# Half of the attention's gate as the first fill beside the last mixer's keys' chain, and the self-attention's rows in another tile

## The chip, the cores and the metric

One Trainium2 chip, one core. The metric is the time of one execution on the device in microseconds; each version is run several times and the median counts.

## The reference, cut to what matters

The whole model is one program: a first block of two layers (recurrent and attention mixers, cross-attention to a memory, MLPs), then a second block: a hybrid mixer and a mixture of 16 experts chosen by the experts. The change lies in the hybrid mixer. There are 256 positions of width 1024; the attention has 8 query and 2 key heads of 64, the delta rule 8 heads of 64 in both directions.

```python
proj = h @ w_in
aq, ak, av, dq, dk, dv, dz, b_raw, a_raw, g_raw = jnp.split(proj, ...)
# self-attention
q = axial_rope(rmsnorm_2(heads(aq, 8), q_norm_w), row, col)
k = axial_rope(rmsnorm_2(heads(ak, 2), k_norm_w), row, col)
attn = block_attention(q, k, heads(av, 2))
# delta rule, forward and backward, in chunks of 64
cq, ck, cv = jnp.split(silu(short_conv(concatenate([dq, dk, dv]), conv_w)), 3)
qd, kd = l2norm(heads(cq, 8)) * 64 ** -0.5, l2norm(heads(ck, 8))
o = rmsnorm_2(o_fwd + o_bwd, dn_norm_w) * silu(dz)
# two gates, then the output
gate_a, gate_d = jnp.split(sigmoid(g_raw), 2)
merged = gate_a * (attn @ w_attn_up) + gate_d * (dn @ w_dn_up)
x = x + gt1 * (merged @ w_o)
```

## The kernel before, in words

A dense product runs as three passes of split operands (L391, L392 and L393: high times high, low times high, high times low); a "dense row" below is one such matmul. Each weight tile of 1 MB comes through SP's queue into a ring of buffers named raw, and is split by ScalarE (L374, whi) and VectorE (L375, wlo). Features stand on the partitions (dense_fm_steps: 128 features by 256 positions) or positions do (dense_tm_steps).

mixer2 (L1184) does the hybrid mixer in four stretches, from about 830 to 1106 us.

- *The keys' chain.* The keys of the delta rule are convolved on TensorE (L1299), squared and summed per head (L1321), normed by Newton steps on VectorE (newton, L458 to L473), scaled (L1330) and transposed (L1335). Beside that decay() makes masks of decays (matmul L1352, multiplication L1357), and products() multiplies keys with keys (L1370) and with the masks (L1374).
- *The inverse*, for two pairs of chunks, pair_a and pair_b (inverse_steps). Each of four levels is a matmul (L1616, in each()), a multiplication on VectorE (L1642), a second L1616, and its result copied by ScalarE (L1646) and transposed by VectorE (L1647); the next level needs both. A last level is L1659 and L1667.
- *The recurrence* over the chunks (rec_steps: L1716 to L1754).
- *The end*: O is normed (L1779 to L1790), transposed (L1793), and goes through w_dn_up; then mixer2_out multiplies by w_o.

These are chains of small steps. All other work of the mixer is a chain of generators, `fill`, pulled at lower priority by counts between the steps of the chains (FILL_K, FILL_A, FILL_B, FILL_R), or up to a flag (until). In order, before: the projection of the delta rule's queries (project(0), with a convolution of sixteen multiply-adds L1181 on VectorE and L1302) and their norm (heads_normed(0): L1317, L1321, newton, L1330, L1335); the projection of self-attention's rows (its epilogue ez3 writes zq); the queries' masks and products; gains_loaded(), which loads the group p2 into finr and makes gt1; rotary() (L1405 to L1440), which reads zq and tab; the values (ev, with eight more L1181); the attention's gate (ega writes a tanh into m1), mixed with attend() (L1453 to L1479); the scaled queries; the attention's up-projection (ea); the two gates of the delta rule; and final_gain(), which multiplies X by finr (L1560). The framework's scheduler sets the final order on each engine from the order of issue and the priorities.

Behind the mixer the experts' weights follow, 192 loads of 1 MB named wx on the same SP queue, each into the next buffer that comes free.

finr and gt1 are two halves of the tile zT, whose earlier contents are used up by then. zq and tab are views of m1, the tile into which the gate is written later.

Of the kernel before, what the change touches and what calls it, by code (L numbers as in the profile page):

```python
# [47 lines left out]
MIX = 3  # L48
# [256 lines left out]
def _body(ctx, tc, I, lay, out, stop):  # L305
# [127 lines left out]
    def dense_tm_steps(W, c0, ncols, a, emit, kc=8, step=512, part=1024):  # L433
        ah, al = a
        for g0 in range(c0, c0 + ncols, step):
            wd = min(step, c0 + ncols - g0)
            kt = 2048 // step
            ws = [weights(W.load(k0 * P, kt, g0, wd), kt, wd, part=part) for k0 in range(0, kc, kt)]
            if step == 256:
                ps = bank_mm().rearrange("p (t n) -> p t n", t=2)  # L440
                ps = [ps[:, t, :] for t in range(2)]
            else:
                ps = [bank_mm() for _ in range(2)]
            for k in range(kc):
                wh, wl = ws[k // kt](k % kt, 0, wd)
                for t in range(2):
                    sl = slice(t * P, (t + 1) * P)
                    mm3(ps[t][:, :wd], ah[:, k, sl], al[:, k, sl], wh, wl, k == 0 and (t == 0 or step != 256),
                        k == kc - 1)
                if k < kc - 1:  # L450
                    yield
            for t in range(2):
                emit(t, g0 - c0, wd, ps[t][:, :wd])
            yield
# [546 lines left out]
    fill = Fill()  # L1001
# [182 lines left out]
    def mixer2(pool, norms):  # L1184
# [6 lines left out]
        W = weight("w_in_2")  # L1191
# [7 lines left out]
        def sc(nm, *shape):  # L1199
            return pool.tile([P] + list(shape or (2, 16)), F32, name=nm)  # L1200

        heads_up.pop()
        a = ah, al = features_tiles()

        rows = act.tile([P, 8, S + 2], F32, name="zT").rearrange("p c t -> p (c t)")
        finr, gt1 = rows[:, 0:D], rows[:, D:2 * D]

        shk = sc("shk", 4)
        for j in range(4):
            nc.scalar.copy(shk[:, j:j + 1], keys[j][:, S:S + 1])  # L1210
# [11 lines left out]
        m1 = pool.tile([P, 8, S], F32, name="m1")  # L1222
# [151 lines left out]
                nc.vector.tensor_tensor(m, hd(ps)[:, 4 * t:4 * t + 4, :], m, OP.mult)  # L1374


        flat = m1.rearrange("p c t -> p (c t)")
        zq = flat[:, 0:1280].rearrange("p (t n) -> p t n", t=2)
        tab = flat[:, 1280:1792].rearrange("p (k t d) -> p k t d", k=4, t=2)
        qT, kT, zv = (held[7][:, a:b].rearrange("p (c t) -> p c t", c=c)  # L1380
                      for a, b, c in ((0, 1024, 4), (1024, 1536, 2), (1536, 1792, 2)))
        sq8 = sc("sq8", 20)
# [142 lines left out]
        def ega(c, nb, ps):  # L1525
            nc.scalar.activation(m1[:, c:c + nb, :], ps, AF.Tanh, scale=0.5)
# [10 lines left out]
        def attention_inside():  # L1537
            for t in range(2):
                for d in range(2):
                    decay(d, t, 1)  # L1540
                    yield
            for hp in range(2):
                products(1, hp)
                yield

        def flag(name):
            done.add(name)
            return
            yield

        def gains_loaded():
            load_group(None, "p2", nc.sync, finr)

            gain_rows(2, 0.5, gt1)
            return
            yield
# [6 lines left out]
        def mix(p, q, n):  # L1563

            for _ in q:
                yield
                for _ in range(n):
                    if next(p, 0) is None:
                        yield
            yield from p  # L1570

        fill = chain(project(0), heads_normed(0),
                     dense_tm_steps(W, 0, 768, a, ez3, step=256), attention_inside(), flag("aT"), gains_loaded(),
                     rotary(), dense_fm_steps(W, 1792, 512, a, ev), flag("v"),
                     mix(dense_fm_steps(W, 2848, 1024, a, ega), attend(), MIX),
                     scaled_queries(), flag("qg"),
                     dense_fm_steps(weight("w_attn_up_2"), 0, D, (at[:, :4, :], at[:, 4:, :]), ea, kc=4),
                     dense_tm_steps(W, 2304, 512, a, ez, step=256), final_gain(),
# [605 lines left out]
```

## Time and profile before

| what | value |
|---|---|
| median of 3 runs | 1592.44 us (1588.39 to 1595.42) |
| profiled execution: its time / its span | 1594.02 / 1592.2 us |
| mean granted TensorE clock | 0.972 |
| TensorE busy | 1452.9 us (91% of the span) |
| VectorE busy | 853.0 us (54%) |
| ScalarE busy | 615.0 us (39%) |
| chain that ended last | TensorE 66%, DMA 25%, VectorE 5%, ScalarE 3% |

Shares are means over stages with different limits. The 25% of DMA in the chain are the experts' weights in the last 470 us; ahead of these the chain is TensorE's nearly throughout. What the change touches is some 280 us of the span, the mixer, so the stretch is read and not the mean.

### The profile page before, as it was taken

To read this page: it belongs to the slowest core of one execution; us is meant where nothing else is said; L and a number is where in the kernel's file an instruction comes from. 1 tells how busy PE (TensorE), PEld (TensorE's weight loads), DVE (VectorE), ACT (ScalarE), POOL (GpSimd) and SP (SyncE) were. 2 spreads that over 40 slices of the span, in tenths; PEclk is the share of its full clock that TensorE was granted. 3 is DMA by queue.
4 is the path that set the end of the run, shared out by engine and by line. 5 is a ranking of instruction groups with operands and counts; after the bars stand their busy time and mean duration, and the time that the engine had idled before them with its cause. 6 is when DMAs were issued, how large, how long until landed. Compare 5 with 4: busy or idle time off the path is not lost.

```text
span 1592.2 us, 25448 instructions
## 1 busy us (share of the span) xinstructions
PE 1452.9 (91%) x10592; PEld 1079.3 (68%) x10592; DVE 853.0 (54%) x1563; ACT 615.0 (39%) x1027; POOL 56.0 (4%) x69
## 2 busy tenths in 40 slices
PE   8999999999999999999999899999988786776776
PEld 8988898889887778898888788899834111111111
DVE  7785667877566766877566986556632001001001
ACT  6655545444445555644444456533311000000000
POOL 0000200000000020000002100010000000000000
PEclk9989999999999999999999999999998997998997
DMA  8535436876553334787544222436899999999998
GB/s 305 208 119 183 158 137 226 314 282 219 187 182 108 106 133 146 271 292 290 191 164 152 81 82 81 151 117 214 350 392 422 423 424 422 422 424 424 422 424 359
DMA packets 58772, 398.23 MB, mean 250 GB/s; under 512 B 6816, under 2 KB 7968, under 8 KB 12064
## 3 DMA queue, kind: packets, MB, share of 16 engines
q1 hardware_dynamic: 57168, 393.10, 64.2%
q10 hardware_dynamic: 1488, 3.49, 0.6%
q8 instruction: 83, 1.36, 0.3%
q14 instruction: 33, 0.27, 0.0%
HBM read 395.52 MB, written 1.05 MB: 249 GB/s over the span
## 4 chain that ended last, share of the span: by engine, by line
PE 66%; DMA 25%; DVE 5%; ACT 3%; issue 1%; SPq 0%; DVEq 0%; ACTq 0%
DMA raw<-in_wx_dram 24%; PE mm L391 14%; PE mm L393 14%; PE mm L392 14%; PE acc L392 3%; PE acc L393 3%; PE acc L391 3%; PE acc L1616 2%; DVE wlo L375 1%; PE mm L1983 1%; PE acc L1983 1%; DMA fraw<-in_w_ada_dram 1%; PE acc L549 1%; ACT whi L374 1%; PE mm L930 1%
## 5 line engine op out<-in xcount | busy, mean ns | idle before, releaser
L375 DVE TENSOR_TENSOR wlo<-raw,whi 128x1024 fp32r<-128x1024 f32 (+1 forms) x299 | 362.4, 1215 | 181.1 <-ACT whi L374 174.4
L374 ACT CAST whi<-raw 128x1024 fp32r<-128x1024 f32 (+1 forms) x299 | 309.6, 1040 | 345.9 <-PE mm L392 170.8
L391 PE MATMUL mm<-hTh,whi 128*128 128x256 f32 x1064 | 300.8, 286 | 6.6 <-ACT whi L374 6.2
L393 PE MATMUL mm<-hTh,wlo 128*128 128x256 f32 x1064 | 301.4, 286 | 4.9 <-DVE wlo L375 4.9
L392 PE MATMUL mm<-hTl,whi 128*128 128x256 f32 x1064 | 302.5, 287 | 0.0
L391 PEld LDWEIGHTS mm<-hTh,whi 128*128 128x128 f32 x1064 | 203.1, 192 | 11.3 <-ACT whi L374 6.2
L393 PEld LDWEIGHTS mm<-hTh,wlo 128*128 128x128 f32 x1064 | 203.6, 192 | 7.9 <-DVE wlo L375 6.8
L392 PEld LDWEIGHTS mm<-hTl,whi 128*128 128x128 f32 x1064 | 203.6, 192 | 1.9 <-issue 1.1
L1983 PE MATMUL mm<-raw,xe 128*32 128x512 f32 x504 | 109.3, 614 | 31.2 <-DMA raw<-in_wx_dram 31.2
L1983 PE MATMUL acc<-raw,xe 128*32 128x512 f32 x512 | 97.5, 608 | 19.1 <-DMA raw<-in_wx_dram 19.1
L1983 PEld LDWEIGHTS mm<-raw,xe 128*32 128x32 f32 x504 | 22.8, 111 | 113.6 <-DMA raw<-in_wx_dram 72.8
L2119 ACT ACTIVATE sgl<-acc 128x512 f32<-128x512 f32 x8 | 4.7, 597 | 215.1 <-PE acc L1983 215.1
L1983 PEld LDWEIGHTS acc<-raw,xe 128*32 128x32 f32 x512 | 21.4, 110 | 89.4 <-DMA raw<-in_wx_dram 51.2
L391 PE MATMUL acc<-whi,hh 128*128 128x512 f32 x192 | 75.7, 394 | 0.0
L392 PE MATMUL acc<-wlo,hh 128*128 128x512 f32 x192 | 75.7, 395 | 0.0
L393 PE MATMUL acc<-whi,hl 128*128 128x512 f32 x192 | 75.0, 394 | 0.0
L2120 DVE SCALAR_TENSOR_TENSOR sgl<-sgl,acc 128x512 f32<-128x512 f32 x8 | 5.4, 686 | 110.2 <-ACT sgl L2119 110.2
L1049 DVE SCALAR_TENSOR_TENSOR macc<-fraw,cs,macc 128x1024 f32<-128x1024 f32 x40 | 51.3, 1282 | 21.5 <-DMA fraw<-in_w_ada_dram 21.2
L2003 DVE SCALAR_TENSOR_TENSOR sgl<-sgl,mm 128x512 f32<-128x512 f32 x8 | 5.5, 688 | 106.0 <-PE mm L1983 105.9
L2016 PE MATMUL acc<-raw,xe 128*32 128x512 f32 x256 | 40.4, 738 | 22.6 <-DMA raw<-in_wx_dram 22.5
L393 PE MATMUL mm<-whi,hTl 128*128 128x256 f32 (+2 forms) x192 | 58.8, 308 | 0.7 <-DVE hTl L554 0.7
L392 PE MATMUL mm<-wlo,hTh 128*128 128x256 f32 (+2 forms) x192 | 58.8, 308 | 0.4 <-DVE wlo L375 0.4
(563 smaller groups left out, 2601.9 us busy)
## 6 DMA issues: line engine op xcount, KB each, us to landing
raw<-in_wx_dram SPq DMA_DIRECT2D x191, 1024.0 KB, 19.8
raw<-in_mlp_w_up_dram SPq DMA_DIRECT2D x32, 1024.0 KB, 5.0
raw<-in_mlp_w_down_dram SPq DMA_DIRECT2D x32, 1024.0 KB, 5.1
fraw<-in_w_ada_dram SPq DMA_DIRECT2D x22, 1024.0 KB, 6.7
raw<-in_w_in_dram SPq DMA_DIRECT2D x19, 1024.0 KB, 4.9
raw<-in_xa_w_kv_dram SPq DMA_DIRECT2D x16, 1024.0 KB, 4.9
raw<-in_ab_w_in_dram SPq DMA_DIRECT2D x9, 1024.0 KB, 8.6
raw<-in_xa_w_q_dram SPq DMA_DIRECT2D x8, 1024.0 KB, 4.7
```

The costliest lines, as they stand in the source:

```text
L374: nc.scalar.copy(hi[:, a:b], raw[:, c0 + a:c0 + b])
L375: (nc.gpsimd if len(parts) in slow else nc.vector).tensor_sub(lo[:, a:b], raw[:, c0 + a:c0 + b], f(hi[:, a:b]))
L391: mm(o, lh, rh, start=start, stop=False, skip_group_check=True)
L392: mm(o, lh, rl, start=False, stop=False, skip_group_check=True)
L393: mm(o, ll, rh, start=False, stop=stop, skip_group_check=True)
L549: mm(o[j * 64:j * 64 + 64, q0:S], v[:, k, vcol:vcol + 64], pT[:, c0:c0 + S - q0], start=k == 0, stop=k == 1, skip_group_check=True)
L930: mm(pss[s][:, c0:c1], qk[rs, qc, q0:q0 + P], qk[rs, kcs[s], 0:kn], start=True, stop=True)
L1049: nc.vector.scalar_tensor_tensor(acc[:, sl], w, ck, acc[:, sl], OP.mult, OP.add)
L1616: mm(o[J, c], lh[J, c], rh[J, c], start=True, stop=True)
L1983: mm(banks[n][j * 32:(j + 1) * 32, :], xe[:, c, g0 + j * 32:g0 + (j + 1) * 32], raw[:, e * D + n * 512:e * D + (n + 1) * 512], start=c == ...
L2003: nc.vector.scalar_tensor_tensor(sg[:, sl], sg[:, sl], 0.5, bu[n], OP.mult, OP.mult)
L2016: mm(by[j * 32:(j + 1) * 32, :], hT[:, c + k, j * 32:(j + 1) * 32], raw[:, k, j, :], start=c + k == 0, stop=c + k == 7, tile_position=(0, ...
```

## The change: what it does

The attention's gate has 1024 features. Its first half (w_in's columns 2848 to 3359) moves from beside attend() to the very front of the fill, ahead of the queries' projection. The second half stays beside attend(). The first half writes m1's first four chunks, which zq and tab occupy at that time before; so these two move to the first 1792 columns of `rows`, the tile zT. There finr and gt1 stand later, so gains_loaded(), which fills these, moves behind rotary(), the last reader of zq. No operation is added or left out.

```diff
         finr, gt1 = rows[:, 0:D], rows[:, D:2 * D]
+        zqt = rows[:, 0:1792]
...
-        flat = m1.rearrange("p c t -> p (c t)")
-        zq = flat[:, 0:1280].rearrange("p (t n) -> p t n", t=2)
-        tab = flat[:, 1280:1792].rearrange("p (k t d) -> p k t d", k=4, t=2)
+        zq = zqt[:, 0:1280].rearrange("p (t n) -> p t n", t=2)
+        tab = zqt[:, 1280:1792].rearrange("p (k t d) -> p k t d", k=4, t=2)
...
-        fill = chain(project(0), heads_normed(0),
-                     dense_tm_steps(W, 0, 768, a, ez3, step=256), attention_inside(), flag("aT"), gains_loaded(),
-                     rotary(), dense_fm_steps(W, 1792, 512, a, ev), flag("v"),
-                     mix(dense_fm_steps(W, 2848, 1024, a, ega), attend(), MIX),
+        fill = chain(dense_fm_steps(W, 2848, 512, a, ega), project(0), heads_normed(0),
+                     dense_tm_steps(W, 0, 768, a, ez3, step=256), attention_inside(), flag("aT"),
+                     rotary(), gains_loaded(), dense_fm_steps(W, 1792, 512, a, ev), flag("v"),
+                     mix(dense_fm_steps(W, 3360, 512, a, lambda c, nb, ps: ega(4 + c, nb, ps)), attend(), MIX),
```

Lines of the changed kernel are two higher than before from L1208 to L1377, and one higher behind that. The counts of pulls are unchanged.

On TensorE, at the end of the keys' chain, this is the order before (L1352 decays, L1335 the keys' transposes, L1370 keys' products, L1317 the queries' transposes; the dense rows behind are self-attention's):

```order
L1352 MATMUL acc<-w_8670,raw_8439 128x512
L1352 MATMUL acc<-w_8678,raw_8439 128x512
L1335 MATMUL tp<-ident,raw_8441 128x128 x4
L1352 MATMUL acc<-w_8857,raw_8439 128x512
L1335 MATMUL tp<-ident,raw_8441 128x128 x4
L1370 MATMUL acc<-raw 64x64 x16
L1317 MATMUL tp<-ident,raw_8435 128x128 x2
L1370 MATMUL acc<-raw 64x64 x16
L1317 MATMUL tp<-ident,raw_8435 128x128 x2
L391 MATMUL mm<-whi,hTh 128x256
L1317 MATMUL tp<-ident,raw_8435 128x128 x4
L391 MATMUL mm<-whi,hTh 128x256
```

and this of the changed kernel, from the same L1352 on (L1354, L1337, L1372; the dense rows are the queries'):

```order
L1354 MATMUL acc<-w_8670,raw_8439 128x512
L1337 MATMUL tp<-ident,raw_8441 128x128 x8
L1354 MATMUL acc<-w_8678,raw_8439 128x512
L1354 MATMUL acc<-w_8827,raw_8439 128x512
L1372 MATMUL acc<-raw 64x64 x32
L391 MATMUL mm<-hTh,whi 128x256
L392 MATMUL mm<-hTl,whi 128x256
```

The queries' L1317 have left this place. The dense rows ahead of it are 96 in both: the queries' before, the gate's first half now.

At the end of pair_a's inverse on TensorE, before (L1616 two levels, with 34 dense rows between them, of which two are shown, then L1659 the last level):

```order
L1616 MATMUL acc<-w_9820,w_9625 64x64 x16
L1616 MATMUL acc<-w_9749,raw_8431 64x64 x16
L1440 MATMUL tp<-ident,raw_8437 128x128
L1440 MATMUL tp<-ident,raw_8435 128x128 x2
...
L391 MATMUL mm<-hTh,whi 128x256
L392 MATMUL mm<-hTl,whi 128x256
L1616 MATMUL acc<-w_9914,w_9750 64x64 x16
L1659 MATMUL acc<-w_9839,raw_8431 32x32 x16
L1496 MATMUL tp<-ident,wf 128x128 x4
```

and in the changed kernel (L1617 for L1616, L1337 and L1372 the queries' transposes and products, L1437 self-attention's transposes, L1660 and L1668 the last level):

```order
L1617 MATMUL acc<-w_9793,w_9557 64x64 x16
L1617 MATMUL acc<-w_9695,raw_8431 64x64 x16
L1337 MATMUL tp<-ident,wf 128x128 x8
L1372 MATMUL mm<-raw 64x64 x16
L1437 MATMUL tp<-ident,raw_8437 128x128
L1617 MATMUL acc<-w_9899,w_9696 64x64 x16
L1660 MATMUL acc<-w_9812,raw_8431 32x32 x16
L1372 MATMUL mm<-raw 64x64 x15
L1668 MATMUL acc<-w_9961,w_9813 32x32 x16
L1660 MATMUL acc<-w_9918,raw_8431 32x32 x16
```

The dense rows between the last levels have gone, and the queries' small matmuls stand there.

On VectorE, between the last two transposes of pair_a's inverse, before (L1647 the transposes, L1181 the values' convolution, L1642 the level's multiplication):

```order
L1647 STREAM_TRANSPOSE w_9840<-acc 128x512
L1181 SCALAR_TENSOR_TENSOR wf<-raw_8443,p_8452,wf 128x256 x2
L1642 TENSOR_TENSOR w_9914<-acc,raw_8439 128x512
L1181 SCALAR_TENSOR_TENSOR wf<-raw_8443,p_8452,wf 128x256 x2
L1175 MEMSET raw_8443 128x2x2
L375 TENSOR_TENSOR wlo<-raw,whi 128x1024
L1492 SCALAR_TENSOR_TENSOR wf<-wf 128x512
L1647 STREAM_TRANSPOSE w_9934<-acc 128x512
```

and in the changed kernel (L1648 and L1643 the same, L1561 final_gain()'s product, L1411 to L1433 rotary()):

```order
L1648 STREAM_TRANSPOSE w_9813<-acc 128x512
L1643 TENSOR_TENSOR w_9899<-acc,raw_8439 128x512
L470 TENSOR_TENSOR nw_a<-nw_y,ss_9562 128x20
L1561 TENSOR_TENSOR X<-X,zT 128x1024 x2
L471 SCALAR_TENSOR_TENSOR nw_b<-nw_a,nw_y 128x20
L473 SCALAR_TENSOR_TENSOR nw_y<-nw_b,nw_y 128x20
...
L473 SCALAR_TENSOR_TENSOR nw_y<-nw_b,nw_y 128x20
L1411 TENSOR_SCALAR sq_8565<-nw_y 128x20
...
L1433 COPY raw_8435<-raw_8435 128x64
L1648 STREAM_TRANSPOSE w_9919<-acc 128x512
```

The values' convolution has gone behind the last transpose, and final_gain()'s two products of 1024 columns and the end of rotary() stand ahead of it.

At the mixer's end the order holds 117 dense rows before between the last L1751 of the recurrence and the first L1793, and 64 in the changed kernel. On SP's queue the load of p2 stood ahead of nine loads of w_in before and stands behind them now, ahead of the four loads of w_attn_up.

## Rows read from the trace of the kernel before

**Rows 1.** TensorE's waits, 850 to 1130 us: who, for whom, total us, times, longest.

```profile
PE tp L1335 <- DVE raw L1330: 2.2, 1, 2.2
PE tp L1317 <- DVE raw L1302: 1.9, 1, 1.9
...
PE tp L1472 <- ACT raw L532: 1.2, 1, 1.2
```

**Rows 2.** Busy time by stretch: us, then PE, PEld, DVE, ACT, POOL, PEclk, DMA share, GB/s.

```profile
870.00:895.00 25.00, 20.06 (x165) 15.88 (x164) 22.03 (x54) 14.38 (x25) 3.00 (x2) 0.87 0.13 44
895.00:950.00 55.00, 54.74 (x864) 49.59 (x863) 48.56 (x107) 25.18 (x44) 4.90 (x4) 0.99 0.30 103
```

**Rows 3.** The same view behind the mixer, two stretches.

```profile
1110.00:1114.00 4.00, 4.00 (x36) 4.00 (x35) 3.27 (x5) 2.63 (x3) 0.00 (x0) 1.00 0.00 2
1200.00:1300.00 100.00, 81.82 (x430) 26.54 (x426) 13.23 (x34) 8.11 (x18) 0.00 (x0) 0.90 1.01 422
```

**Rows 4.** Timeline of TensorE, 874 to 904 us: start, us, line, tile.

```profile
874.16 1.02 PE L1352 MATMUL acc<-w,raw 128*128 128x512 f32 x2
...
882.65 1.91 PE L1352 MATMUL acc<-w,raw 128*128 128x512 f32 x2
...
901.24 1.15 PE L1616 MATMUL acc<-w,raw 64*64 64x64 f32 x32
```

**Rows 5.** Timeline of VectorE, 870 to 906 us.

```profile
872.57 0.53 DVE L1324 TENSOR_SCALAR ss<-ss 128x16 f32<-128x16 f32 x1
...
881.00 1.29 DVE L1330 TENSOR_TENSOR raw<-raw,ss 128x512 f32<-128x512 f32 x2
...
904.96 0.18 DVE L471 SCALAR_TENSOR_TENSOR nw_b<-nw_a,nw_y 128x16 f32<-128x16 f32 x1
905.17 0.18 DVE L473 SCALAR_TENSOR_TENSOR nw_y<-nw_b,nw_y 128x16 f32<-128x16 f32 x1
```

**Rows 6.** VectorE by line, 845 to 950 us: count, busy us, mean ns, idle before.

```profile
L375 DVE TENSOR_TENSOR wlo<-raw,whi 128x1024 fp32r<-128x1024 f32 x13 | 15.9, 1221 | 3.1 <-ACT whi L374 3.1
L1181 DVE SCALAR_TENSOR_TENSOR raw<-raw,p 128x256 f32<-128x256 f32 x16 | 7.1, 476 | 0.0
L1647 DVE STREAM_TRANSPOSE w<-acc 128x512 f32<-128x512 f32 x8 | 5.7, 712 | 3.7 <-ACT w L1646 3.7
...
L1181 DVE SCALAR_TENSOR_TENSOR wf<-raw,p,wf 128x256 f32<-128x256 f32 x8 | 3.4, 475 | 0.2 <-ACT wf L1179 0.2
...
L1374 DVE TENSOR_TENSOR raw<-mm,raw 128x256 f32<-128x256 f32 x8 | 2.9, 416 | 0.0
...
L1560 DVE TENSOR_TENSOR X<-X,zT 128x1024 f32<-128x1024 f32 x2 | 2.4, 1224 | 0.2 <-DMA zT<-in_p_dram 0.2
...
L1429 DVE TENSOR_TENSOR raw<-raw,nw_y 128x128 f32<-128x128 f32 x2 | 1.0, 482 | 0.0
...
L1431 DVE COPY raw<-raw 128x64 f32<-128x64 f32 x2 | 0.7, 342 | 0.0
```

**Rows 7.** VectorE from the keys' norms to the first pair's end, as in rows 2.

```profile
871.00:950.00 79.00, 73.80 (x1018) 64.47 (x1017) 70.15 (x159) 38.56 (x67) 7.91 (x6) 0.96 0.25 86
```

**Rows 8.** Timeline of TensorE at the mixer's end.

```profile
1087.70 1.14 PE L1751 MATMUL acc<-w,raw 64*64 64x64 f32 x16
...
1100.03 0.28 PE L391 MATMUL mm<-hTh,whi 128*128 128x256 f32 x1
1100.15 0.28 PE L392 MATMUL mm<-hTl,whi 128*128 128x256 f32 x1
...
1102.91 1.03 PE L1793 MATMUL tp<-ident,w 128*128 128x128 f32 x8
```

**Rows 9.** Timeline of VectorE at the mixer's end.

```profile
1095.48 1.23 DVE L375 TENSOR_TENSOR wlo<-raw,whi 128x1024 fp32r<-128x1024 f32 x1 [0.74 <-ACT whi L374]
...
1100.01 1.28 DVE L1790 TENSOR_TENSOR w<-w,wf 128x512 f32<-128x512 f32 x2
```

**Rows 10.** Transfers of 840 to 1000 us: count, KB, median us to landing.

```profile
zT<-in_p_dram SPq DMA_DIRECT2D x1, 512.0 KB, 3.5
```

## Prediction

> **What bounds the kernel now.** I read the windows first, stage by stage, to see where a microsecond is worth a microsecond. Behind the mixer the experts' weights bind: 423 GB/s and a DMA share of 1.01 while TensorE is four fifths busy, but at 1110 to 1114 us the same share is 0.00 [rows 3]. The stream cannot start before the mixer and the output product have given back their weight buffers. So a shift of the mixer's end passes on to the end one for one, as long as no load is brought forward.
>
> Inside the mixer TensorE binds: 54.7 of 55 us at 895 to 950. The exception is the keys' chain at 870 to 895, where TensorE is busy for 20.1 of 25 us and VectorE for 22.0, at a granted clock of 0.87 [rows 2]. The waits name the places: 2.2 us before L1335 (the keys' transposes, for VectorE's L1330) and 1.9 us before L1317 (the queries' transposes, for L1302) [rows 1]. In all TensorE idles 4.9 us in that window, 25 less 20.1. The timeline shows what the clock does behind an idle: a pair of L1352 takes 1.02 us at 874 and 1.91 us just behind the 2.2 us wait [rows 4]; that is the lower of the two levels, 1.2 GHz. A mean of 0.87 over 25 us means some 6.5 us at that level, and half of it is lost, 3.3 us. So the keys' chain loses **8.2 us** in all. That is all this change can win there.
>
> Why is L1330 late? VectorE's timeline: the Newton steps of the keys' norm begin behind L1324 at 872.57, and L1330 starts at 881.00, 8.4 us later. Undisturbed, Newton steps follow each other every 0.21 us [rows 5]. Between them stand the queries' sixteen convolution steps L1181, 7.1 us [rows 6].
>
> **The change part by part.** No operation is added or removed; the sum of matmul time between the mixer's ends is the same. Only places move.
>
> *Keys' chain.* The first gate half stands where the queries' projection stood: the same 96 dense rows, ahead of the same L1352. It has no VectorE epilogue (one tanh on ScalarE), so the sixteen L1181 and one L1302 leave the Newton steps. From 872.57: L1324 0.5, eleven steps of 0.21, one L1357 of 0.7, and hand-over: L1330 starts at about 876.5 to 877 instead of 881.0. Then the rest of the chain (L1352, the eight transposes, ScalarE's copies, L1370) still has no dense row among it. Going through it row by row leaves TensorE about 1.8 us idle, and the second wait, for L1302, is gone. **Gain 8.2 − 1.8 = 6.4 us**, bounded by 8.2 (no idle) and 4.
>
> *First inverse.* The queries' VectorE work is not gone. It stands in the first pair's inverse, in which every L1616 waits for VectorE's L1642 or L1647. That stretch was full already: 70.2 of 79.0 us from 871 to 950 [rows 7]. Counting by the order what stands ahead of the last L1647: eight L1181 of the values (3.4), eight L1374 (2.9), L1492 (0.65, as each L1330 [rows 5]) and two small copies (0.2 each) leave, 7.4 in all; two L1560 (2.4, which stood in an idle place before) and one L375 (1.2) come in [rows 6]. That leaves 66.4 us of work. With the old 8.8 us of gaps the last L1647 would end 3.8 us earlier than before: the **lower bound** of the sum for both parts, and a gain.
>
> The upper one comes from the last three steps. Before, 27 to 34 dense rows stood between two steps of the inverse on TensorE, and VectorE had 5 to 6 us of work per step; each covered the other. Now the last three steps hold 11 dense rows, then none. VectorE between the last two L1647 has L1560 2.4, L1429 1.0, the copies L1431 and L1432 some 1.3, ten small steps of 0.21, and L1642 with L1647 1.4 [rows 5, 6]: about 8 us. TensorE has beside it two L1616 of 1.1 [rows 4], the queries' transposes and products, and L1659: about 4.8. So it waits 3.2 us; the same sums for the two steps ahead (6.9 against 4.3, 8.9 against 6.7) give 2.6 and 2.2. **Cost 8.0 us**, at TensorE's most exposed. Both parts together: −6.4 + 8.0 = **+1.6**, between −3.8 and +2. I take the upper end, because the order gives TensorE nothing to do in these steps. The lower needs the gaps not to grow while the covers shrink.
>
> *Attention.* Half of the gate was the filler beside attend(); now 96 dense rows stand there, not 192, and they run out in the first of four rounds. The one wait of that kind was 1.2 us (L1472 for ScalarE's softmax) [rows 1]; I expect one more, of that size or a little less: **+0.8**, from 0 to 2.
>
> *Tail.* The last recurrence step (L1751) ends at 1088.84; the norm chain on ScalarE and VectorE lets L1793 begin once the first L1790 is done, at 1100.65 [rows 8, 9]. That is 11.8 us, under 117 dense rows of 0.12 us [rows 8], 13.9 us: no wait before. Now 64 rows are left, 7.6 us. The chain has the same three L375 in it; 0.7 us of it is a wait for ScalarE's cast that TensorE sets [rows 9], and may go. So TensorE waits 11.8 − 0.7 − 7.6 = **3.5 us** in front of L1793, bounded by 0 (if the recurrence itself runs ahead) and 4.2. Behind L1793 stand the delta rule's up-projection and then the output product, whose buffers the stream waits for.
>
> *The load of p2 (zT, 512 KB).* On SP's queue it moves behind nine weight loads and waits for the last reader of zq, and the four loads of the attention's up-projection stand behind it. It lands 3.5 us after its start [rows 10]. By the order VectorE has some 6 us of work between that reader and L1560. So it costs nothing; without that cover it would stall VectorE up to 3.5 us in the inverse. The rows' new place costs nothing: tile zT is free until then, and the writes and reads keep their sizes.
>
> *Clock behind the new idles.* Waits of 2.2 and 1.9 us cost 3.3 us by the lower level in the keys' chain. The new ones of 2.2 to 3.5 us may do the same, but behind them stand small matmuls: 0 to 3.4 us, taken as 0.5.
>
> The Trainium skill (Perfetto Trace Analysis, Matmul Optimizations) says that the matmul engine scales its power with its use, so that matmuls should run back to back. By that rule alone, closing the chain's two waits would be worth the whole 8.2 us, and 1592 would become 1584. The trace agrees with its mechanism (a pair of L1352 at 1.91 against 1.02 us), but the rule counts only the waits that close, and the order opens others; its result is the full gain among the rivals.
>
> **Sum.** +1.6 + 0.8 + 3.5 + 0.5 = +6.4 us on the profiled 1594.0, which stands 1.6 above the median 1592.4. On the median that is 1598.8. Three of four terms are at the exposed end, so I take a little off: **1598 us**.
>
> **The rivals.** A difference of 8 us (0.5%) is about what this kernel's measurement can tell from none.
> - *Covers hold (faster side).* The inverse's gaps stay at 8.8 us: −3.8, the recurrence runs ahead so that the tail does not wait, attention +0: 1588 to 1589. For it: VectorE really has less work there. Against: 64 rows for a chain of 11 us. To gain over 8 us it would need the whole 8.2 with nothing given back: 1584. Decides: the wait before the last L1659 is under 1 us.
> - *All waits exposed and the clock falls behind each (slower side).* +2.0, +2 in attention, +4.2, +3.4 of clock: +11.6, 1604. For it: the two waits of before both did it. Decides: granted clock under 0.9 behind the inverse and at L1793.
> - *The p2 load is late.* 3.5 us more on VectorE in the inverse: 1601 to 1602. Against: the cover of 6 us.
> - *Nothing arrives, since the stream binds.* If weight buffers, not the mixer, set its start, the time stays 1592. Against: the share of 0.00 at 1110.
>
> **Chances.** Forecast (+3 to +8) 0.45; covers hold in part or whole (−4 to +3) 0.25, a full gain over 8 us 0.05; all exposed 0.15; late load 0.05; nothing arrives 0.05. Of the forecast's 0.45 I put 0.1 over 8 us, since a median of three runs moves by 3 us. So slower by over 0.5%: 0.1 + 0.15 + 0.05 = 0.30; faster: 0.05; same: 0.65. The range is 1588 (covers hold) to 1604 (all exposed).
>
> **What would show it.** Right: L1330 at about 877 and no wait for L1302; waits of over 2 us at the end of the first inverse, released by VectorE; TensorE idle some 3.5 us before L1793. Wrong: dense rows or short waits in these places, or a tail in which the recurrence's last step comes several us earlier than 1087.7.

## The result and the profile after

The changed kernel takes 1611.16 us (median of 7 runs, 1602.65 to 1612.82) against 1593.21 for the kernel before (7 runs, 1588.39 to 1597.27): the recorded ratio is 1.0091 [1.0073, 1.011], some 14.5 us slower, while the two medians stand 18.0 us apart. The forecast was 1598 with a range up to 1604: the sign of its sum was right, the size was not.

The profiled execution of the changed kernel took 1612.82 us, with a span of 1611.0 and a granted clock of 0.960. Ahead of the mixer the two programs are alike, but this execution reaches the mixer's first products 3.6 us later; so 3.6 is taken off when a time of after is set against one of before.

Two tables of windows cut the mixer into the same five stages: up to the first product of the inverse, the first pair's inverse, from there to the end of the recurrence, the wait and dense rows before the last transposes, and on to the first output product of w_o. Columns as in rows 2. The kernel before:

```profile
845.70:901.24 55.54, 48.86 (x356) 41.70 (x355) 43.82 (x96) 29.79 (x60) 13.05 (x16) 0.94 0.23 86
901.24:949.40 48.16, 47.91 (x805) 42.92 (x805) 41.73 (x98) 22.34 (x39) 2.85 (x2) 1.00 0.28 93
949.40:1088.84 139.44, 137.63 (x1924) 122.90 (x1920) 80.31 (x140) 67.10 (x137) 7.57 (x8) 1.00 0.35 120
1088.84:1102.91 14.07, 14.07 (x117) 14.07 (x118) 11.72 (x23) 6.26 (x8) 0.00 (x0) 1.00 0.77 276
1102.91:1128.60 25.69, 23.54 (x194) 22.89 (x193) 17.48 (x25) 11.86 (x17) 0.00 (x0) 1.00 0.64 240
```

The changed kernel:

```profile
849.30:900.12 50.82, 47.20 (x363) 41.72 (x361) 36.04 (x76) 26.28 (x52) 11.91 (x18) 0.97 0.29 98
900.12:953.02 52.90, 48.45 (x823) 43.87 (x822) 45.18 (x98) 23.64 (x43) 4.13 (x4) 0.94 0.28 97
953.02:1109.70 156.68, 148.22 (x1946) 133.22 (x1946) 88.99 (x163) 70.98 (x145) 8.98 (x9) 0.96 0.30 103
1109.70:1121.01 11.31, 7.87 (x65) 7.67 (x65) 9.35 (x22) 5.29 (x7) 0.00 (x0) 1.00 1.02 409
1121.01:1147.30 26.29, 25.83 (x191) 25.41 (x192) 16.98 (x25) 10.50 (x15) 0.00 (x0) 0.87 0.53 191
```

By stage that is −4.7, +4.7, **+17.2**, −2.8 and +0.6: together +15.1 (298.0 against 282.9). The keys' chain gained and the inverse gave it back; most of the loss lies in the third stage, where attention, the second inverse and the recurrence run.

The stages are cut at steps of the chains, and dense rows have moved across the cuts. The first four hold 201, 160, 513 and 64 dense rows now, and 186, 171, 464 and 117 before. The third stage's rows of the first pass (L391), before and in the changed kernel, show it (window, length, PE, PEld, granted clock, DMA share, GB/s):

```profile
949.40:1088.84 139.44, 44.30 (x155) 28.99 (x155) 1.00 0.35 120
953.02:1109.70 156.68, 49.18 (x171) 32.95 (x171) 0.96 0.30 103
```

So the third stage has 49 rows more and the fourth 53 fewer. With 0.12 us for a row [rows 8], an estimate of the change by stage for equal work is −6.5, +6.1, **+11.4** and +3.6.

TensorE's busy time with the same work is 277.6 instead of 272.0, so 5.6 us of the loss are longer busy time and 9.5 are idle time. By stage the idle time changes by −3.1, +4.2, +6.6, +3.4 and −1.7. Behind the mixer nothing has changed: 463.6 us remained to the span's end (1592.2 − 1128.6), and now 463.7 (1611.0 − 1147.3).

TensorE's waits of the changed kernel, 845 to 1150 us (who, for whom, total us, times, longest):

```profile
PE tp L1473 <- ACT raw L532: 4.6, 4, 1.3
PE acc L1617 <- DVE w L1643: 4.2, 2, 4.0
PE tp L1794 <- DVE w L1791: 3.4, 1, 3.4
PE mm L393 <- DVE wlo L375: 1.7, 1, 1.7
...
PE acc L1617 <- ACT w L1682: 1.4, 1, 1.4
PE acc L1660 <- DVE w L1648: 1.1, 1, 1.1
```

Both waits of the keys' chain [rows 1] have gone, and one for the cast L375 (1.7) has come there. The new waits are those for the softmax (L1473, four times), in the first inverse (L1617 for L1643, and L1660) and at the end (L1794). What the clock does behind such waits is seen in three stretches of the changed kernel (windows, columns as in rows 2):

```profile
941.00:946.00 5.00, 4.01 (x66) 3.83 (x67) 5.00 (x14) 0.58 (x1) 0.00 (x0) 0.50 0.32 105
953.00:960.00 7.00, 6.21 (x54) 6.03 (x54) 3.46 (x11) 2.14 (x6) 1.80 (x1) 0.55 0.01 2
1119.00:1126.00 7.00, 4.53 (x20) 4.13 (x21) 4.16 (x8) 1.46 (x5) 0.00 (x0) 0.64 0.84 331
```

Granted are 0.50 and 0.55 in the inverse and 0.64 at the end, so mostly the lower level, 1.2 GHz, while TensorE has work. TensorE's timeline in the inverse shows the same in durations (start, us, line, tile):

```profile
941.96 1.97 PE L1617 MATMUL acc<-w,w 64*64 64x64 f32 x32 [3.97 <-DVE w L1643]
943.72 1.92 PE L1617 MATMUL acc<-w,raw 64*64 64x64 f32 x32
...
948.62 1.15 PE L1617 MATMUL acc<-w,w 64*64 64x64 f32 x32
...
953.79 1.73 PE L1660 MATMUL acc<-w,raw 32*32 32x32 f32 x32 [1.07 <-DVE w L1648]
```

The same 32 matmuls take 1.97 us behind the wait of 3.97 and 1.15 a little later. VectorE's timeline of the changed kernel:

```profile
880.29 1.29 DVE L1332 TENSOR_TENSOR raw<-raw,ss 128x512 f32<-128x512 f32 x2
...
946.87 0.71 DVE L1648 STREAM_TRANSPOSE w<-acc 128x512 f32<-128x512 f32 x1
...
948.15 2.35 DVE L1561 TENSOR_TENSOR X<-X,zT 128x1024 f32<-128x1024 f32 x2
...
953.02 0.71 DVE L1648 STREAM_TRANSPOSE w<-acc 128x512 f32<-128x512 f32 x1
...
992.08 0.68 DVE L1678 TENSOR_TENSOR w<-raw,beta 128x512 f32<-128x512 f32 x1
...
998.33 0.69 DVE L1634 TENSOR_TENSOR w<-raw,raw 128x512 f32<-128x512 f32 x1
```

against the same two last steps in the kernel before:

```profile
967.60 0.69 DVE L1677 TENSOR_TENSOR w<-raw,beta 128x512 f32<-128x512 f32 x1
...
977.75 0.68 DVE L1633 TENSOR_TENSOR w<-raw,raw 128x512 f32<-128x512 f32 x1
```

L1678 scales the values for pair_a's last products; it is 20.9 us later (992.1 − 3.6 − 967.6). L1634 begins the second pair's inverse, 17.0 us later. The first inverse itself ends at 953.0 − 3.6 = 949.4, to the tenth of a microsecond where it ended before.

### The profile page after: what moved, and what is told of

It is laid out like the page before. It is cut to its first block, busy times and chain, and to the rows that moved or that the text cites. A ratio compares the mean times of both kernels' runs of the same rounds, so it can differ in the third digit from the quotient of the medians.

```text
span 1611.0 us, 25457 instructions
## 1 busy us (share of the span) xinstructions
PE 1462.3 (91%) x10592; PEld 1090.7 (68%) x10592; DVE 855.4 (53%) x1563; ACT 614.3 (38%) x1027; POOL 56.0 (3%) x69
## 4 chain that ended last, share of the span: by engine, by line
PE 65%; DMA 25%; DVE 5%; ACT 3%; issue 1%; SPq 0%; ACTq 0%; DVEq 0%
DMA raw<-in_wx_dram 23%; PE mm L393 14%; PE mm L391 14%; PE mm L392 14%; PE acc L392 3%; PE acc L393 3%; PE acc L391 3%; PE acc L1617 2%; DVE wlo L375 1%; PE mm L1984 1%; DMA fraw<-in_w_ada_dram 1%; PE acc L1984 1%; PE acc L549 1%; ACT whi L374 1%; PE mm L930 1%
## 5 line engine op out<-in xcount | busy, mean ns | idle before, releaser
L375 DVE TENSOR_TENSOR wlo<-raw,whi 128x1024 fp32r<-128x1024 f32 (+1 forms) x299 | 362.3, 1215 | 198.5 <-ACT whi L374 189.1
L391 PE MATMUL mm<-hTh,whi 128*128 128x256 f32 x1064 | 303.5, 289 | 6.6 <-ACT whi L374 6.2
L393 PE MATMUL mm<-hTh,wlo 128*128 128x256 f32 x1064 | 304.2, 288 | 5.9 <-DVE wlo L375 5.8
L393 PEld LDWEIGHTS mm<-hTh,wlo 128*128 128x128 f32 x1064 | 206.3, 195 | 9.9 <-DVE wlo L375 8.0
L391 PEld LDWEIGHTS mm<-hTh,whi 128*128 128x128 f32 x1064 | 206.2, 195 | 9.7 <-ACT whi L374 6.2
L391 PE MATMUL acc<-whi,hh 128*128 128x512 f32 x192 | 75.7, 394 | 0.0
L393 PE MATMUL acc<-whi,hl 128*128 128x512 f32 x192 | 75.0, 394 | 0.0
L393 PE MATMUL mm<-whi,hTl 128*128 128x256 f32 (+2 forms) x192 | 58.2, 305 | 0.0
```

Source lines behind the costliest of these rows:

```text
L375: (nc.gpsimd if len(parts) in slow else nc.vector).tensor_sub(lo[:, a:b], raw[:, c0 + a:c0 + b], f(hi[:, a:b]))
L391: mm(o, lh, rh, start=start, stop=False, skip_group_check=True)
L393: mm(o, ll, rh, start=False, stop=stop, skip_group_check=True)
```

## The experiments

There are four theories; the letters are those of the expectations. **Clock** (K): a wait of some 3 us drops TensorE to 1.2 GHz, and it stays there long after, so each wait costs more than itself. **Values** (V): the 96 dense rows of the gate at the front make the values' projection late; pair_a's end draws the fill up to them (until), TensorE burns its dense rows meanwhile, and these then lack beside the softmax and at the end. **Rows' place** (P): p2's load, gain_rows and the two products L1561 come into the inverse and load VectorE there. **Attend's cover** (C): half as many rows stand beside the softmax and are pulled too early, or attend() itself comes later. Ratios are against the kernel before in the same series; its medians there lay between 1594.4 and 1595.0.

**e1: the rows' new place alone**, with the old order of the fill (whole gate beside attend).

```diff
-        fill = chain(dense_fm_steps(W, 2848, 512, a, ega), project(0), heads_normed(0),
+        fill = chain(project(0), heads_normed(0),
...
-                     mix(dense_fm_steps(W, 3360, 512, a, lambda c, nb, ps: ega(4 + c, nb, ps)), attend(), MIX),
+                     mix(dense_fm_steps(W, 2848, 1024, a, ega), attend(), MIX),
```

> The fill stands in its old order (whole gate beside attend, queries first); only the rows' new place and the later load of p2 stay. Theory V (the half gate ahead of everything puts the values' projection later, and the first pair's last products and the second pair's inverse wait for the values): the values come as before, so the time is that of the kernel before within 0.3% (1588 to 1598 us), with the keys' chain's two waits back. Rival P (the rows' place: p2 lands late, and final_gain's two products of 1.2 us stand in the inverse): 3 to 8 us of the loss stay, 1597 to 1602 us.

1610.19 us, 1.0091 [1.0062, 1.0119]: as slow as the whole change, and above what either theory expected. Its inverse has one long wait; TensorE's timeline:

```profile
948.64 1.15 PE L1617 MATMUL acc<-w,w 64*64 64x64 f32 x32 [2.89 <-DVE w L1643]
```

and its windows from there on:

```profile
940.00:950.00 10.00, 6.67 (x141) 6.19 (x138) 10.00 (x28) 3.81 (x8) 0.14 (x1) 1.00 0.33 108
950.00:970.00 20.00, 20.00 (x165) 14.63 (x163) 8.99 (x25) 10.30 (x27) 0.00 (x0) 0.51 0.16 53
```

VectorE is full at 940 to 950, TensorE waits; then it is busy 20.00 of 20 us at a clock of 0.51. Half of 20 us is some 10 us lost, by estimate, behind a wait of 2.9.

**e2: one piece of six dense rows behind each step of attend() instead of three pieces**, in the changed kernel.

```diff
-MIX = 3
+MIX = 1
```

> The changed kernel with the second gate half spread over attend, one piece of six dense rows behind each of its steps instead of three (MIX 1 for 3). Rival C (cover: the loss is the waits beside attend and at the mixer's end, because the dense rows run out there): the waits for the softmax shrink from 4.6 to under 2 us, and with the clock that they cost the time falls by 6 to 10 us, to 1599 to 1604 us. Theory V: the chain is late already when attend runs, and rows that are spent here are missing at the end (36 left in front of the last transposes for 64): 1605 to 1612 us, the wait in front of L1794 longer than 3.4 us by what the others shrink.

1617.89 us, 1.0151 [1.0122, 1.0181], slower still, and above both ranges. The waits for the softmax shrink from 4.6 to 1.1 us, but others grow:

```profile
PE tp L1794 <- DVE w L1791: 5.4, 1, 5.4
PE tp L1497 <- DVE wf L1493: 4.9, 1, 4.9
...
PE tp L1473 <- ACT raw L532: 1.1, 3, 0.4
```

So the cover beside attend() is not the whole cause: with the rows spread, the lack appears elsewhere.

**e3: the values ahead of self-attention's rows**, in the changed kernel.

```diff
-        fill = chain(dense_fm_steps(W, 2848, 512, a, ega), project(0), heads_normed(0),
+        fill = chain(dense_fm_steps(W, 2848, 512, a, ega),
+                     project(0), heads_normed(0),
+                     dense_fm_steps(W, 1792, 512, a, ev), flag("v"),
...
-                     rotary(), gains_loaded(), dense_fm_steps(W, 1792, 512, a, ev), flag("v"),
+                     rotary(), gains_loaded(),
```

> The changed kernel with the values' projection moved in the fill from behind rotary to ahead of self-attention's rows; the half gate stays first. Theory V: the values are there before the first pair's inverse is over, the second pair starts at about 960 instead of 995 us, the gain of the keys' chain (4.7 us) stays: 1585 to 1595 us, and no wait in front of the last transposes. Rival C: attend has the same half gate and comes later still, so its waits stay or grow: 1603 to 1612 us.

1607.87 us, 1.0068 [1.0044, 1.0091]. The values' scaling starts at 952.8, and no wait stands before the last transposes any more. But others do:

```profile
PE acc L1619 <- DVE w L1680: 3.4, 1, 3.4
```

A second wait on L1619 takes 2.0 us. Behind them stands the lower level:

```profile
960.00:980.00 20.00, 14.13 (x203) 12.62 (x204) 16.29 (x45) 5.28 (x12) 0.23 (x1) 0.51 0.17 52
```

The softmax's waits are 1.6 us in all and not 4.6, with the same half gate beside attend(). But in time early values win back too little to be told from nothing (the intervals overlap): self-attention comes later, and the clock falls in another place.

**e4: final_gain()'s two products on GpSimd**, in the changed kernel.

```diff
-                nc.vector.tensor_mul(X[:, t, :], X[:, t, :], finr)
+                nc.gpsimd.tensor_mul(X[:, t, :], X[:, t, :], finr)
```

> The changed kernel with final_gain's two products of 128 by 1024 on GpSimd instead of VectorE, so VectorE has 2.4 us less in the last step of the first pair's inverse. Rival P: the time falls by 2 to 5 us, as the inverse ends earlier and the clock stays up. Theory V: the first pair waits for the values for 30 us behind that anyway, so nothing changes: within 2 us of the changed kernel.

1613.49 us, 1.0115 [1.0087, 1.0143]; the waits stand at 4.6, 4.2 and 3.4 us as in the changed kernel, and L1660's is 2.0. But the edit did not free VectorE. GpSimd's products run from 942.67 to 947.84, and two Newton steps on VectorE end about when each of the two does:

```profile
942.67 5.17 POOL L1561 TENSOR_TENSOR X<-X,zT 128x1024 f32<-128x1024 f32 x2 [11.99 <-DMA zT<-in_p_dram]
944.42 1.13 DVE L470 TENSOR_TENSOR nw_a<-nw_y,ss 128x20 f32<-128x20 f32 x1
945.59 2.28 DVE L471 SCALAR_TENSOR_TENSOR nw_b<-nw_a,nw_y 128x20 f32<-128x20 f32 x1
947.91 0.18 DVE L473 SCALAR_TENSOR_TENSOR nw_y<-nw_b,nw_y 128x20 f32<-128x20 f32 x1
```

The same steps take 0.18 us right behind. So e4 does not decide what these products cost.

**e5: e1 with four throw-away matmuls in the place of its wait**; their result is overwritten by the product that follows.

```diff
+                    if lev == 4 and (d, t) == (1, 1):
+                        for _ in range(4):
+                            mm(pm[:, :S], M[0, 0][:, :P], M[0, 0][:, :S], start=True, stop=True)
```

> The kernel of e1 (only the rows' place and the later load of p2) with four matmuls of 128 by 256 that compute nothing needed, put on TensorE exactly into the one long wait (2.9 us) ahead of the last second-level product of the first pair's inverse. They add some 1.5 us of work. Theory K (clock: e1 loses 10 of its 11.5 us because TensorE runs 20 us at the lower level behind that wait): the level does not fall there, 8 to 10 us come back, 1594 to 1602 us. Rival P (what costs is the chain itself, late by VectorE's extra work): the matmuls change nothing or cost 1 to 2 us, 1608 to 1612 us, and the level is low behind that place as before.

1594.77 us, 1.0001 [0.9984, 1.0019]: the whole loss of e1 is gone. The timeline has the throw-away matmuls where the wait was (the eight of L1647), and the product after them at 949.29 instead of 948.64:

```profile
946.34 2.00 PE L1647 MATMUL acc<-w 128*128 128x256 f32 x8 [0.87 <-ACT w L1650]
```

The inverse is no faster for it. The windows show where most of the 15 us come from:

```profile
940.00:950.00 10.00, 8.68 (x154) 7.77 (x152) 10.00 (x29) 3.54 (x6) 0.00 (x0) 1.00 0.32 108
950.00:970.00 20.00, 19.43 (x269) 16.41 (x265) 13.59 (x31) 15.47 (x37) 0.71 (x1) 1.00 0.25 80
```

In the same 20 us TensorE does 269 matmuls at 1.00 instead of 165 at 0.51. The two kernels have TensorE's steps in the same order up to that place; behind it some of attend()'s steps stand elsewhere. The clock theory is shown for the rows' place, with e11 as its control. The Trainium skill (Perfetto Trace Analysis, Matmul Optimizations) asks for matmuls back to back, since the engine scales its power with its use. Filling the wait agrees with that, 269 matmuls against 165. That the clock stayed at 0.51 in e1, with TensorE busy in 20.00 of 20 us, does not follow from it.

**e6: the rows in a tile of their own**, and gains_loaded() back ahead of rotary(): the new order of the fill alone.

```diff
-        zqt = rows[:, 0:1792]
+        zqt = pool.tile([P, 1792], F32, name="zqo")
...
-                     dense_tm_steps(W, 0, 768, a, ez3, step=256), attention_inside(), flag("aT"),
-                     rotary(), gains_loaded(), dense_fm_steps(W, 1792, 512, a, ev), flag("v"),
+                     dense_tm_steps(W, 0, 768, a, ez3, step=256), attention_inside(), flag("aT"), gains_loaded(),
+                     rotary(), dense_fm_steps(W, 1792, 512, a, ev), flag("v"),
```

> The fill's order of the change (half gate first), but self-attention's rows in a tile of their own, so that p2's load and its gains stay where they are in the kernel before. Theory V (the values come some 11 us of dense rows later, and the first pair waits for them): the waits in the inverse, beside attend and at the end stay, 1604 to 1611 us. Rival P (the rows' place is the whole loss): the keys' chain's gain is left alone, 1586 to 1594 us.

1604.35 us, 1.0058 [1.0037, 1.008]. The waits are those of the changed kernel (4.6, 4.5 and 3.4). So by the ratios the order alone costs more than half of the loss. Taking p2's work out of the inverse has not shortened the inverse's wait of 4.0.

**e7 and e8: the values first, and the gate, rows and values ahead of the queries**, both with the tile of e6.

```diff
+        fill = chain(dense_fm_steps(W, 1792, 512, a, ev), flag("v"),
+                     dense_fm_steps(W, 2848, 512, a, ega),
+                     project(0), heads_normed(0),
+                     dense_tm_steps(W, 0, 768, a, ez3, step=256), attention_inside(), flag("aT"), gains_loaded(),
+                     rotary(),
```

> Own tile for the rows; the fill begins with the values' projection, then the half gate, then the queries and self-attention's rows. Theory V with K: the values are there 30 us before they are asked for, the inverse has 14 to 37 dense rows between its steps, and the level falls only where a wait is left: 1584 to 1594 us. If attend, which then comes 30 us later, is what bounds (rival C): waits for the softmax at the end of attend and 1598 to 1608 us.

```diff
+        fill = chain(dense_fm_steps(W, 2848, 512, a, ega),
+                     dense_tm_steps(W, 0, 768, a, ez3, step=256),
+                     dense_fm_steps(W, 1792, 512, a, ev), flag("v"),
+                     project(0), heads_normed(0),
+                     attention_inside(), flag("aT"), gains_loaded(),
+                     rotary(),
```

> Own tile; the fill is the half gate, self-attention's rows, the values, then the queries. The values come ahead of the inverse's end and the queries' VectorE work is out of both the keys' chain and the inverse. Theory V with K: 1582 to 1592 us, with the keys' chain's gain kept. Rival C: the queries' products come last and hold the recurrence's first step; attend is no earlier than in e7: 1596 to 1606 us.

1607.28 us, 1.0076 [1.0055, 1.0097], as rival C had it, and 1610.97, 1.0097 [1.0073, 1.012], above both ranges. In e7 the longest waits are 3.5 us (L1619, for VectorE's L1680) and 3.2 (L1497); in e8 GpSimd's L1352 and the softmax hold TensorE:

```profile
PE mm L1354 <- POOL wf L1352: 5.9, 2, 3.4
PE tp L1473 <- ACT raw L532: 2.6, 2, 2.4
```

In each order tried, a chain waits for the part that is put off.

**e9 and e10: the changed kernel, and e6, with throw-away matmuls** in the inverse's wait and before the last transposes (`last` is the squares' tile, made just ahead).

```diff
+                    if lev == 4 and (d, t) == (0, 0):
+                        for _ in range(7):
+                            mm(pm[:, :S], M[1, 1][:, :P], M[1, 1][:, :S], start=True, stop=True)
...
+            for _ in range(7 if t == 0 else 0):
+                mm(pt[:, :S], last[:, :P], last[:, :S], start=True, stop=True)
```

> The changed kernel with seven matmuls of 128 by 256 that compute nothing needed ahead of the seventh second-level product of the first pair's inverse (where TensorE waits 4.0 us for VectorE) and seven ahead of the last transposes (3.4 us wait). Theory K+V (of the 15 us lost in the mixer some two thirds is the lower level of the clock behind those waits, the rest waits because the chain is late): 6 to 10 us come back, 1599 to 1605 us, not the whole. If the chain's lateness is all (theory V alone): 1608 to 1612 us. If the clock is all (theory K alone): 1592 to 1597 us.

> The same two groups of matmuls in the kernel of e6 (half gate first, rows in their own tile, p2 early). Theory K+V: e6 lost some 6 us by the clock behind the same two waits, so 4 to 6 us come back, 1597 to 1601 us; theory V alone: 1604 to 1607 us; theory K alone: 1588 to 1595 us.

1605.95 us, 1.0063 [1.0043, 1.0084], and 1605.48, 1.0062 [1.0039, 1.0086]. e9 lies between two of its three ranges, e10 where the values alone would put it. In both the waits for L1643 and L1791 are no longer among the long ones; the softmax's stays at 4.6, and a new one comes:

```profile
PE tp L1337 <- DVE wf L1332: 2.1, 1, 2.1
```

(e9's wait.) By the ratios the changed kernel gets back some 0.3 points of its 0.9, though the intervals overlap, and e6 nothing. So about a third of the change's loss seems to hang on the clock behind those two waits together with the rows' place, and what is left is the order's: e6, e9 and e10 agree at 0.6. The values' scaling is at 985.3 in e9, with its mixer 1.2 us late: still 16.5 us later than before.

**e11: the kernel before with e5's four matmuls**, to see what they do by themselves.

```diff
+                    if lev == 4 and (d, t) == (1, 1):
+                        for _ in range(4):
+                            mm(pm[:, :S], M[0, 0][:, :P], M[0, 0][:, :S], start=True, stop=True)
```

> Control: the kernel before with the four matmuls of e5 at the same place of the first pair's inverse, where it has dense rows and no wait. Theory K: nothing to win, they cost their own 2 us or hide: 1593 to 1598 us. If the matmuls helped by themselves (an order that happens to be better): 1586 to 1591 us.

1596.10 us, 1.0004 [0.9989, 1.0019]: nothing. What e5 wins is the wait's clock.

**e12: the kernel before with the gate's first half right ahead of the values**, all else in its old place; so the values come late while keys' chain and first inverse stay as they were.

```diff
-                     rotary(), dense_fm_steps(W, 1792, 512, a, ev), flag("v"),
-                     mix(dense_fm_steps(W, 2848, 1024, a, ega), attend(), MIX),
+                     rotary(),
+                     dense_fm_steps(W, 2848, 512, a, ega),
+                     dense_fm_steps(W, 1792, 512, a, ev), flag("v"),
+                     mix(dense_fm_steps(W, 3360, 512, a, lambda c, nb, ps: ega(4 + c, nb, ps)), attend(), MIX),
```

> The kernel before with one edit: the half gate stands in the fill just ahead of the values instead of beside attend. The rows stay in m1, p2 stays early, the queries stay first, the keys' chain and the first pair's inverse keep their dense rows. Theory V (96 dense rows ahead of the values hold the first pair's last products, and with them the second pair, by some 15 us): 1600 to 1607 us as in e6 and e10, first products with the values at 980 to 988 us, and waits beside attend and of 3 to 4 us before the last transposes. Rival D (what is left in e10 comes from the queries' VectorE work in the first inverse): no more than 1597 us.

1602.25 us, 1.0047 [1.0034, 1.0059]. Its waits:

```profile
PE tp L1472 <- ACT raw L532: 4.6, 4, 1.3
PE tp L1795 <- DVE w L1792: 3.4, 1, 3.4
```

These are the changed kernel's waits for the softmax and at the end, to the tenth. The values' scaling begins at 981.97 instead of 967.60. So 96 dense rows ahead of the values are enough for most of e6's 0.58%, with nothing else of the change. The edit also takes these rows from beside attend(). That the late values and not the missing rows make the softmax's waits is argued from e3 and e13: there the half gate stands beside attend() too, the values are early, and these waits are 1.6 and 1.4 us.

**e13: the values between two parts of self-attention's rows**, with e6's tile.

```diff
+                     dense_tm_steps(W, 0, 512, a, ez3, step=256),
+                     dense_fm_steps(W, 1792, 512, a, ev), flag("v"),
+                     dense_tm_steps(W, 512, 256, a, lambda t, n0, wd, ps: ez3(t, n0 + 512, wd, ps), step=256),
+                     attention_inside(), flag("aT"), gains_loaded(),
```

> The kernel of e6 (half gate first, rows in their own tile) with the values' projection moved ahead of the last 96 rows of self-attention's projection, so that it stands where it stood counted in dense rows. Theory V: the values come by 965 us or earlier and the loss of e6 shrinks to the clock behind what waits are left: 1592 to 1600 us, no wait before the last transposes. Rival C or D: attend comes later by the same rows, and the waits beside it bound: 1604 to 1612 us.

1605.53 us, 1.0067 [1.0044, 1.0089]: no better than e6. The values are early and the end has no wait, but self-attention is later, with waits of 2.3 us (L1437) and 1.5 (L1441), and the clock falls twice:

```profile
964.00:978.00 14.00, 11.67 (x191) 10.58 (x189) 10.65 (x35) 4.18 (x9) 0.00 (x0) 0.52 0.01 2
1022.00:1036.00 14.00, 13.08 (x144) 10.07 (x144) 4.00 (x9) 6.60 (x18) 0.00 (x0) 0.52 0.17 69
```

Bringing the values back does not bring the time back, so late values are not all that an order can cost.

The runs lose in two ways, as one window over the mixer shows, from the first stage's start to the end of the fifth (e1, e6, e12, e13; one profiled execution each):

```profile
845.71:1139.90 294.19, 281.70 (x3384) 250.25 (x3384) 196.78 (x380) 137.46 (x260) 25.63 (x31) 0.95 0.35 122
843.86:1136.70 292.84, 273.52 (x3385) 247.13 (x3385) 196.04 (x380) 136.94 (x261) 22.17 (x26) 0.97 0.35 123
845.26:1135.60 290.34, 272.07 (x3385) 246.33 (x3385) 193.85 (x379) 137.08 (x261) 28.68 (x25) 0.97 0.35 124
845.88:1138.80 292.92, 280.97 (x3385) 251.72 (x3385) 195.74 (x380) 137.01 (x261) 26.55 (x25) 0.95 0.35 123
```

Against the kernel before (282.9 us, 272.0 of them busy, 10.9 idle):

| run | busy, us | idle, us |
|---|---|---|
| e1, the rows' place alone | +9.7 | +1.6 |
| e6, the order alone | +1.5 | +8.4 |
| e12, the half gate ahead of the values | +0.1 | +7.4 |
| e13, values early | +9.0 | +1.1 |
| the whole change | +5.6 | +9.5 |

The number of matmuls is the same within 2. Late values cost waiting; the rows' place and the early values of e13 cost busy time, with long stretches at a clock of 0.51 or 0.52. The whole change has both.

## Why the prediction fell short

The forecast's sum was +6.4 us and the mixer took 15.1 more. In the sum, the waits that close and open make +9.2 (−3.1 + 8.0 + 0.8 + 3.5), and the clock −2.8 (3.3 back in the keys' chain, 0.5 lost behind the new idles). Measured are +9.5 of idle time and +5.6 of busy time. So the sum of the waits came out right, by luck: one term was too high and another too low by more. Nearly the whole miss, 8.4 of 8.7 us, is busy time, which the stretches at 0.50 to 0.64 put down to the clock. Two steps failed, the clock's and attention's.

- **Clock behind the new idles: the step that failed in the sum.** It was taken as 0.5 us, from 0 to 3.4, with the reason that only small matmuls stand behind. In its place the busy time rises by 5.6, though the keys' chain runs at a higher clock. In e1 some 10 us are lost behind one wait, as the lower level lasts 20 us there and reaches dense rows. Filling two of the change's waits gave back some 0.3% (e9).
- **Attention: the step that failed among the waits.** It was put at +0.8, from 0 to 2, by counting which dense rows are left beside attend(). The waits for the softmax rose from 1.2 [rows 1] to 4.6, a 1.4 for L1682 came, and the stage to the recurrence's end has 6.6 us more idle time. I asked what TensorE has to do there, and not what the 96 rows at the front make late: 96 × 0.12 us [rows 8] is 11.5 us by itself, and it stands ahead of the values, for which pair_a waits and, behind it, the second inverse. The half gate right ahead of the values costs 0.47% by itself, some 7.5 us (e12).
- **Keys' chain: right.** L1332 starts at 880.3 − 3.6 = 876.7, forecast 876.5 to 877. The idle time falls by 3.1, as forecast, though what is left stands in another place: 1.7 us before L393, for VectorE's wlo. The stage is 4.7 us shorter and holds 15 dense rows more, so it gains some 6.5 for equal work; the forecast was 6.4. One reading was wrong without entering the sum: of the sixteen L1181, ten and not all stand between L1324 and L1330 in VectorE's timeline of before (4.35 us and not 7.1).
- **First inverse: right in kind, too high.** Forecast were three waits of 2.2, 2.6 and 3.2 (8.0); two came, 4.0 and 1.1, and the stage has 4.2 us more idle time. Between the last two L1648 VectorE needs 953.02 − 946.87 = 6.2 us and not 8, so the last wait is 1.1 and not 3.2. Both parts as cut give 0.0 (forecast +1.6, bounds −3.8 to +2).
- **Load of p2: right for the stall, wrong that its place costs nothing.** It lands in time: L1561 runs at 948.15 without a wait. But e1 puts +0.9% on the rows' place alone, through VectorE's work in the inverse, one wait and the clock. In the whole change it counts, by the ratios, for the third that e6 lacks, and by the profiles for 4.1 us of busy time; the two losses do not add.
- **Tail: right.** The wait before L1794 is 3.4 us, forecast 3.5. As 53 rows fewer stand there, the stage is shorter all the same; those rows were spent earlier.

The nearest rival was "all waits exposed and the clock falls": its condition came true in part (0.50 to 0.55 in the inverse, 0.64 at L1794), and its price of 3.4 us for the clock, which stood for all waits together, was too low as well.

**What stays open.** What work, and how much, brings the level back is not settled by these runs. In e1, whether the products L1561 or gain_rows weigh more was not separated, and e4 does not settle it. No run delays the values and leaves the whole gate beside attend(), so how e12's loss divides between the two is argued and not shown. How the losses of the order and of the rows' place combine is seen but not explained. Whether e3, e7 or e13 with all their waits filled would beat the kernel before was not tried; no version here does, and e5 only equals it.

## What to carry to other kernels

When dense work is moved ahead, list what stands behind it in the same queue and which chain is waiting for that; a fully busy TensorE hides that a value comes 20 us late. When dense work has moved across the cuts between stages, compare the stages for equal work, and split the loss into idle time and busy time before naming a cause. Price a new wait of 3 us on TensorE by the granted clock of the whole stretch behind it, not by its own length. Where such a wait can't be removed, a few throw-away matmuls in it are a cheap test of what the clock takes.

## What the runs showed of the hardware

One wait of 2.9 us was followed by 20 us at a granted clock of 0.51, though TensorE was busy in 20.00 of these 20 us (e1). Four throw-away matmuls in that wait made it 1.00 and gave back 15 us of the kernel's time (e5), and did nothing where there was no such wait (e11: 1.0004). In the changed kernel a longer wait, 3.97 us, was followed by a clock of 0.50 only until before 948.62, where 32 matmuls take 1.15 us again; that is 6.7 us behind the wait. So how long the lower level lasts is not fixed by the wait's length alone.

Two Newton steps of VectorE that take 0.18 us elsewhere took 1.13 and 2.28 us while GpSimd multiplied 128 by 1024 elements beside them, and each ended with one of GpSimd's products (e4).
